# Where the streamed operand of a weight product lies in SBUF: a layer stack on one core

## The chip, the cores and the metric

The kernel runs on one core of a Trainium2 chip. The metric is the device time of one execution in microseconds; the time before is the median of three runs. One more execution was taken with the hardware profiler, and all rows of the trace come from that one.

## The reference, cut to what matters

Two transformer blocks over 256 positions of width 2048, in float32. The first block has a mixer (stick-breaking attention on 8 heads and a gated delta rule on 8 heads, joined by `w_out`), a cross attention to 256 memory positions, and a feed-forward part with a short convolution. The second has a forgetting attention (`fox`) and a sliding-window attention (`swa`). What costs the time are the products of an activation with a weight matrix:

```python
proj = h @ w_in[l]                                # 2048 x 7184
x = x + mixed @ w_out[l]                          # 2048 x 2048
u = causal_dwconv(h @ w_up, conv_w) + conv_b      # 2048 x 11264
y = (jax.nn.silu(gate) * up) @ w_down             # 5632 x 2048
p = h @ fox_w_in[j]                               # 2048 x 8224
x = x + y @ w_out                                 # 2048 x 2048, after fox and after swa
p = h @ swa_w_in[j]                               # 2048 x 4608
```

and the smaller `w_xq`, `w_xkv`, `w_xo` of the cross attention.

## The kernel before, in words

Activations lie transposed, 128 features on the partitions and 256 positions along the free axis. Every operand of a weight product is split into a high part (rounded to `float32r`) and a low part (what is left). `split` writes both parts of an activation tile side by side into one tile of 2 x 256 words, 2,048 bytes a partition. `granules` loads four such blocks of weights by one DMA of SyncE into `wt`, and ACT and DVE make the high and the low part of them in `w2`.

`linB` then makes 256 rows of a product. For each tile of the activation (index k) and each half j of the weight columns there are two matmuls: one streams all 512 columns (high and low part) of the activation tile past the high part of the weights, and one streams the 256 high columns past the low part. So the high part of the weights is loaded into TensorE once for both parts of the activation. I call the two a pair: one matmul of 512 columns, one of 256, each with its own load of 128 x 128 weights. `linA` has the operands the other way round: the activation tile is loaded and `w2` is streamed. It makes the value rows of the attentions.

The activation tiles that are streamed have four names. `xh` (made by `new_x` and `fox_x`, pool `xp`) is the normed input of a block, 16 tiles, used by every product that reads the model width. `mix` (pool `mixp`) holds the outputs of the mixers for `w_out`. `mv` (pools `mvx`, `mvf`, `mva`) holds what goes into `w_xo`, `w_down` and the two later `w_out`. `mm` is the normed memory.

Where they lie follows from the sizes. Pools are laid one behind the other in the order in which they are opened, each with its buffers one behind the other; tiles made through the class `Lined` are rounded up to multiples of 128 bytes. In front of the first pool the program keeps 16,512 bytes a partition. Pool `cp` has 25,344 bytes, pool `wp` has four `wt` of 4,096 and four `w2` of 8,192. So each `w2` begins 128 bytes behind a multiple of 256, and so does the first `xh` tile, at 91,008. An `xh` tile has room for 2,560 bytes, and `x_tile(k)` starts its 2,048 bytes 32 k bytes into it:

```python
t = xp.tile([P, 640], F32R, tag="xh", name="xh")
return t[:, 8 * k : 8 * k + 512].rearrange("p (a b) -> p a b", a=2)
```

Counted in 256s, the `xh` tiles k = 0 to 7 start at 128, 160, 192, 224, 0, 32, 64 and 96, and k = 8 to 15 again so. The tiles of `mix`, `mm` and `mv` all start at 128, as every `w2` does; the steps inside `w2` are multiples of 512 bytes and change nothing in that count.

The order of the work is the order in which the program is written, engine by engine. Side work (attention scores, the delta rule, norms) is held in generators; `tick` moves them on once for each granule of four weight blocks, so its matmuls stand between those of the weight products.

Of the kernel before, what the change touches and what calls it, by code (L numbers as in the profile page):

```python
# [9 lines left out]
F32 = mybir.dt.float32  # L10
F32R = mybir.dt.float32r
# [5 lines left out]
S, D, P = 256, 2048, 128  # L17
# [84 lines left out]
(CONSTS, CAT), (CONSTS_B, BAT), (CONSTS_L, LAT) = _consts()  # L102


LINE = 128


class Lined:
# [5 lines left out]
    def tile(self, shape, dtype, **kw):  # L114
        n, size = int(np.prod(shape[1:])), 2 if dtype == BF16 else 4
        if n * size % LINE == 0:
            return self.pool.tile(shape, dtype, **kw)
        t = self.pool.tile([shape[0], -(-n * size // LINE) * LINE // size], dtype, **kw)[:, :n]
        return t.rearrange("p (a b) -> p a b", a=shape[1]) if len(shape) == 3 else t
# [3 lines left out]
def body(ctx: ExitStack, tc: tile.TileContext, d: dict, out: bass.AP, stop=None):  # L123
# [3 lines left out]

    cp = Lined(ctx.enter_context(tc.tile_pool(name="cp", bufs=1)))
    wp = Lined(ctx.enter_context(tc.tile_pool(name="wp", bufs=4)))
    xp = Lined(ctx.enter_context(tc.tile_pool(name="xp", bufs=16)))  # L130
    sp = Lined(ctx.enter_context(tc.tile_pool(name="sp", bufs=2)))
    pl = ctx.enter_context(tc.tile_pool(name="pl", bufs=2, space=PSUM))
# [2 lines left out]
    def mm(o, lhsT, rhs, start, stop):  # L135
        nc.tensor.matmul(o, lhsT, rhs, start=start, stop=stop, skip_group_check=True)  # L136

    def side(shape, name):
        t = pside.tile([P, 512], F32, tag="side", name=name)
        n = int(np.prod(shape[1:]))  # L140
        v = t[:, :n]
        if len(shape) == 3:
            v = v.rearrange("p (a b) -> p a b", a=shape[1])
        return v

    def tt(o, a, b, op):
        vec.tensor_tensor(o, a, b, op=op)  # L147

    def stt(o, a, s, b, op0, op1):
        vec.scalar_tensor_tensor(o, a, s, b, op0=op0, op1=op1)  # L150
# [14 lines left out]
    def C(name):  # L165
        o, n = CAT[name]
        return cst[:, o : o + n]

    def V(name):
        o, n = COLS[name]  # L170
        return cols[:, o : o + n]
# [35 lines left out]
    def split(mv, src, scale=None):  # L207

        if scale is None:
            act(mv[:, 0, :], src, AF.Copy)  # L210
            tt(mv[:, 1, :], src, mv[:, 0, :].bitcast(F32), ALU.subtract)
        else:
            act(mv[:, 0, :], src, AF.Copy, scale=scale)  # L213
            stt(mv[:, 1, :], src, scale, mv[:, 0, :].bitcast(F32), ALU.mult, ALU.subtract)
# [151 lines left out]
        later("norm", work())  # L366
        return c

    def x_tile(k):

        t = xp.tile([P, 640], F32R, tag="xh", name="xh")
        return t[:, 8 * k : 8 * k + 512].rearrange("p (a b) -> p a b", a=2)

    def new_x(k, g):
        mv = x_tile(k)
        split(mv, XT[:, k, :], V(g)[:, k : k + 1])
        return mv

# [11 lines left out]
    def then(norm, g):  # L390
        xs = []

        def after(k):
            xs.append(new_x(k, g))
            norm.add(XT[:, k, :])

        return xs, after
# [6 lines left out]
    def popen(**kw):  # L404
        cm = tc.tile_pool(**kw)
        p = Lined(cm.__enter__())
        opened.append((p, cm))
        return p
# [16 lines left out]
    def first_x(k):  # L425
        n = 2 if k < 4 else 4
        if k % n == 0 and k not in made:
            src = d["xT"][k * P : (k + n) * P, :].rearrange("(k p) s -> p k s", p=P)
            nc.sync.dma_start(XT[:, k : k + n, :], src)
        if k not in made:  # L430
            made[k] = new_x(k, "mix_norm")
        return made[k]

    xh = [lambda k=k: first_x(k) for k in range(KT)]

    win = d["w_in"]
    mixpool = popen(name="mixp", bufs=16)
    mixed = [None] * 16
    gd = popen(name="gd", bufs=1)
    gates = {}  # L440
    r1 = c1 = None
# [90 lines left out]
    def gdn(hp):  # L532
        nonlocal r1, c1
        KQ = gd.tile([P, 2, 2, 256], F32, tag="KQ", name="KQ")
        if hp:
            for qk, seg in ((1, 0), (0, 1)):
                silu(KQ[:, qk], conv(linB(win, [(0, xh)], 3072 + 1024 * seg + 256 * hp), 8 * seg + 2 * hp))
        else:
            pq = linB(win, [(0, xh)], 3072, (2, 2, 4, 4, 4))
            norm0 = Norm("mix")  # L540
            later("norm", squares(norm0))
            r1 = norm0.rstd(0)
            pk = linB(win, [(0, xh)], 4096, (4, 4))
            nc.sync.dma_start(cols[:, 16:], d["cols"][:, 16:])
            tg = thin(d["w_gates"], V("mix_norm"))
        ps = linB(win, [(0, xh)], 5120 + 256 * hp)
        if hp == 0:
            silu(KQ[:, 1], conv(pq, 0))
            silu(KQ[:, 0], conv(pk, 8))
            nc.sync.dma_start(cst[:], d["consts"])  # L550
            late_constants()
            c1 = column(r1)
            later("gdn", make_gates(tg))
        v = conv(ps, 16 + 2 * hp)
        silu(v[:], v)
        ps = linB(win, [(0, xh)], 6144 + 256 * hp)
        z = t2("y", "z", 2)
        scaled(z[:], ps, r1)
        sz = t2("sz", "sz", 2)
        silu(sz[:], z)  # L560
        later("gdn", chain(hp, KQ, v, sz))

    def chain(hp, KQ, v, sz):
# [162 lines left out]
        for f in range(2):  # L726
            stt(szv[:, :, HALF[f]], ops[:, :, HALF[1 - f]], V("gdn_norm"), szv[:, :, HALF[f]], ALU.mult, ALU.mult)
        for h in range(2):
            mv = mixpool.tile([P, 2, 256], F32R, tag="mix", name="mix")
            split(mv, sz[:, h, :])  # L730
            mixed[8 + 2 * hp + h] = mv

# [13 lines left out]
    def head(hp, h, q, k, vr):  # L746
        if True:
            zt = side([P, 384], "zps")
            dg = zt.rearrange("p (a b) -> p a b", a=3)[:, 0::2, :]
            mm(zt[:, 0:256], k[:, h, 0:128], q[:, h, :], True, False)  # L750
            mm(zt[:, 256:384], k[:, h, 128:256], q[:, h, 128:256], False, False)
            e = gd.tile([P, 384], F32, tag="gt", name="sbe", bufs=4)
            spt = gd.tile([P, 384], F32, tag="gt", name="sbs", bufs=4)
            act(e[:], zt, AF.Abs)
            act(e[:], e[:], AF.Exp, scale=-1.0)
            act(e[:], e[:], AF.Ln, bias=1.0)
            stt(spt[:], zt, 0.0, e[:], ALU.max, ALU.add)
            yield
            sdg = spt[:].rearrange("p (a b) -> p a b", a=3)[:, 0::2, :]
            tt(sdg, sdg, C("sbmask").unsqueeze(1).to_broadcast([P, 2, P]), ALU.mult)  # L760
            mm(zt, C("negl"), spt[:], False, False)
            mm(zt[:, 128:256], C("negones"), spt[:, 256:384], False, False)
            mm(dg, identb[:], sbnegb.unsqueeze(1).to_broadcast([P, 2, P]), False, True)
            w = gd.tile([P, 384], F32, tag="gt", name="sbw", bufs=4)
            act(w[:], zt, AF.Exp)
            yield
            ops_ = side([P, 256], "sbo")
            mm(ops_, vr[:, 0, h * P : h * P + P], w[:, 0:256], True, False)
            mm(ops_[:, 128:256], vr[:, 1, h * P : h * P + P], w[:, 256:384], False, True)
            mv = mixpool.tile([P, 2, 256], F32R, tag="mix", name="mix")  # L770
            split(mv, ops_)
            mixed[2 * hp + h] = mv

# [3 lines left out]
    xh, after = then(norm, "xattn_norm")  # L777
# [10 lines left out]
    def new_mv():  # L788
        return mvbox[0].tile([P, 2, 256], F32R, tag="mv", name="mv")
# [25 lines left out]
    with tc.tile_pool(name="xa", bufs=2) as xa_:  # L815
# [60 lines left out]
        xh, after = then(norm, "ffn_norm")  # L876
# [15 lines left out]
    fx = []  # L892

    def fox_x(k):
        mv = x_tile(k)
        split(mv, XT[:, k, :], fg[:, k : k + 1])
        fx.append(mv)
        norm.add(XT[:, k, :])
        norm2.add(XT[:, k, :], V("final_norm")[:, k : k + 1])

    cw, cb = V("ffn_conv"), V("ffn_conv_bias")
    with tc.tile_pool(name="ff", bufs=2) as ff_:
# [15 lines left out]
        for n in range(22):  # L918
# [6 lines left out]
            for j in range(2):  # L925
                mv = new_mv()
# [9 lines left out]
    xh = fx  # L936
# [176 lines left out]
    for gidx in range(8):  # L1113
        c0 = 256 * gidx
        q = ap_.tile([P, 2, 256], F32, tag="qk", name="q")
        k = ap_.tile([P, 2, 256], F32, tag="qk", name="k")
# [23 lines left out]
    xh, after = then(norm, "norm_g_2b")  # L1140
# [40 lines left out]
    for gidx in range(8):  # L1181
# [4 lines left out]
        for j in range(2):  # L1186
# [4 lines left out]
            h = 4 * gidx + 2 * j  # L1191
# [51 lines left out]
def build(arrays, stop=None):  # L1243
    import concourse.bacc as bacc

    nc = bacc.Bacc("TRN2", target_bir_lowering=False, num_devices=1)
    d = {n: nc.dram_tensor(f"in_{n}", a.shape, F32, kind="ExternalInput").ap() for n, a in arrays.items()}
    out = nc.dram_tensor("out_0", (D, S), F32, kind="ExternalOutput").ap()
    with tile.TileContext(nc) as tc:
        body(tc, d, out, stop)  # L1250
    return nc
# [9 lines left out]
```

## Time and profile before

| what | value |
|---|---|
| time, median of three runs | 2243.81 us (2242.81 to 2244.35) |
| time of the profiled execution | 2246.18 us |
| its span, first to last instruction | 2244.3 us |
| TensorE (PE) busy | 2204.7 us, 98% of the span, 13,582 matmuls |
| loads of weights into TensorE (PEld) busy | 1904.0 us, 85% |
| VectorE (DVE) busy | 1611.4 us, 72% |
| ScalarE (ACT) busy | 1256.5 us, 56% |
| DMA engines, queue of SyncE | 53.5% |

Busy time of an engine is the time in which at least one of its instructions was under way. Matmuls overlap: one starts while the one before it still drains, so the mean duration of a matmul in a row is longer than the distance from its start to the next start. The distance between starts is what a product costs; it is read from the start of one run of matmuls to the start of the next, divided by their count.

### The profile page before, as it was taken

To read this page: it belongs to the slowest core of one execution; us is meant where nothing else is said; L and a number is where in the kernel's file an instruction comes from. 1 tells how busy PE (TensorE), PEld (TensorE's weight loads), DVE (VectorE), ACT (ScalarE), POOL (GpSimd) and SP (SyncE) were. 2 spreads that over 40 slices of the span, in tenths; PEclk is the share of its full clock that TensorE was granted. 3 is DMA by queue.
4 is the path that set the end of the run, shared out by engine and by line. 5 is a ranking of instruction groups with operands and counts; after the bars stand their busy time and mean duration, and the time that the engine had idled before them with its cause. 6 is when DMAs were issued, how large, how long until landed. Compare 5 with 4: busy or idle time off the path is not lost.

```text
span 2244.3 us, 35514 instructions
## 1 busy us (share of the span) xinstructions
PE 2204.7 (98%) x13582; PEld 1904.0 (85%) x13582; DVE 1611.4 (72%) x2681; ACT 1256.5 (56%) x2149; POOL 113.5 (5%) x161
## 2 busy tenths in 40 slices
PE   9999999999999999999999999999999999999997
PEld 7888888878878888888888888888888888888886
DVE  8757666467687766767775778867676666788775
ACT  7545555455565544544553556656556655577652
POOL 1100010000000000000000000000010000000011
PEclk9999999999999999999999999999999999999999
DMA  7443444346546566656666656555555556545453
GB/s 252 146 141 124 141 133 144 120 140 197 180 146 189 187 183 193 190 182 194 188 184 192 188 181 189 175 169 169 172 166 175 164 179 188 160 151 161 158 161 122
DMA packets 110265, 380.06 MB, mean 169 GB/s; under 512 B 11920, under 2 KB 18192, under 8 KB 110096
## 3 DMA queue, kind: packets, MB, share of 16 engines
q1 hardware_dynamic: 108720, 375.96, 53.5%
q8 instruction: 106, 1.74, 0.3%
q10 hardware_dynamic: 1232, 1.06, 0.1%
q0 software_dynamic: 144, 0.79, 0.1%
q14 instruction: 63, 0.52, 0.1%
HBM read 375.66 MB, written 2.10 MB: 168 GB/s over the span
## 4 chain that ended last, share of the span: by engine, by line
PE 92%; DVE 4%; ACT 2%; issue 1%; DMA 1%; POOL 0%; SPq 0%; DVEq 0%; ACTq 0%; POOLq 0%
PE linb L136 77%; PE lina L136 7%; PE zps L136 2%; PE yps L136 1%; PE ptps L988 1%; DVE w L147 1%; PE nps L136 1%; PE wsp L136 1%; DVE XT L150 1%; PE xps L136 1%; ACT w L258 1%; PE snp L136 0%; POOL e L506 0%; DMA MT<-in_memT 0%; PE mps L136 0%
## 5 line engine op out<-in xcount | busy, mean ns | idle before, releaser
L136 PE MATMUL linb<-xh,w 128*128 128x512 f32 x7104 | 1288.9, 340 | 12.0 <-DVE xh L150 3.0
L136 PEld LDWEIGHTS linb<-xh,w 128*128 128x128 f32 x7104 | 1091.9, 189 | 169.6 <-ACT w L258 4.4
L147 DVE TENSOR_TENSOR w<-wt,w 128x1024 fp32r<-128x1024 f32 (+2 forms) x713 | 868.3, 1220 | 325.9 <-ACT w L258 322.8
L258 ACT ACTIVATE w<-wt 128x1024 fp32r<-128x1024 f32 (+2 forms) x713 | 744.6, 1046 | 591.7 <-PE linb L136 429.3
L136 PE MATMUL linb<-mv,w 128*128 128x256 f32 (+1 forms) x2560 | 457.0, 340 | 4.4 <-DVE XT L150 4.2
L136 PEld LDWEIGHTS linb<-mv,w 128*128 128x128 f32 x2560 | 391.7, 188 | 65.9 <-issue 4.2
L136 PE MATMUL lina<-w,xh 128*128 128x512 f32 x832 | 155.2, 342 | 0.7 <-DVE w L147 0.7
L136 PEld LDWEIGHTS lina<-w,xh 128*128 128x128 f32 x832 | 128.1, 188 | 19.3 <-DVE w L147 0.9
L150 DVE SCALAR_TENSOR_TENSOR XT<-linb,XT 128x512 f32<-128x512 f32 x128 | 87.8, 690 | 32.0 <-PE linb L136 30.0
L150 DVE SCALAR_TENSOR_TENSOR y<-pre,cols,y 128x256 f32<-128x256 f32 x248 | 103.3, 479 | 0.2 <-ACT y L518 0.2
L136 PE MATMUL linb<-mix,w 128*128 128x512 f32 (+1 forms) x512 | 93.5, 342 | 1.9 <-DVE mix L147 1.9
L136 PEld LDWEIGHTS linb<-mix,w 128*128 128x128 f32 x512 | 79.6, 191 | 13.3 <-DVE mix L147 2.1
L288 ACT ACTIVATE pre<-linb 128x512 f32<-128x512 f32 x56 | 33.5, 599 | 94.9 <-PE linb L136 94.9
L150 DVE SCALAR_TENSOR_TENSOR pre<-linb,pre 128x512 f32<-128x512 f32 x56 | 38.6, 690 | 48.4 <-ACT pre L288 48.4
L912 ACT ACTIVATE y<-pre,cols 128x256 f32<-128x256 f32 x88 | 48.2, 594 | 26.7 <-DVE pre L147 26.7
L1040 POOL CAST kd<-kd 64x512 fp32r<-64x512 f32 x32 | 32.6, 1020 | 351.6 <-PE lina L136 320.8
L147 DVE TENSOR_TENSOR sqacc<-sqacc,sq 128x256 f32<-128x256 f32 x118 | 48.2, 419 | 1.4 <-DVE fg L147 0.5
L907 POOL MEMSET pre<- 128x4 f32 x44 | 4.3, 103 | 873.7 <-DVE y L150 661.3
L330 ACT ACTIVATE sq<-XT 128x256 f32<-128x256 f32 x90 | 35.5, 404 | 15.1 <-DVE XT L150 12.8
L147 DVE TENSOR_TENSOR pre<-pre,rstd 128x512 f32<-128x512 f32 x56 | 38.7, 691 | 1.6
L213 ACT ACTIVATE xh<-XT,cols 128x256 fp32r<-128x256 f32 x64 | 30.9, 500 | 8.9 <-DVE XT L150 8.8
L136 PE MATMUL zps<-kd,qs 128*128 128x256 f32 x192 | 31.3, 295 | 0.6 <-DVE qs L147 0.6
(300 smaller groups left out, 1573.7 us busy)
## 6 DMA issues: line engine op xcount, KB each, us to landing
wt<-in_w_up SPq DMA_DIRECT2D x176, 512.0 KB, 4.0
wt<-in_fox_w_in SPq DMA_DIRECT2D x128, 512.0 KB, 3.9
wt<-in_w_in SPq DMA_DIRECT2D x111, 512.0 KB, 3.6
wt<-in_swa_w_in SPq DMA_DIRECT2D x72, 512.0 KB, 3.7
wt<-in_w_down SPq DMA_DIRECT2D x64, 512.0 KB, 3.7
wt<-in_w_out SPq DMA_DIRECT2D x32, 512.0 KB, 4.3
wt<-in_fox_w_out SPq DMA_DIRECT2D x32, 512.0 KB, 3.6
wt<-in_swa_w_out SPq DMA_DIRECT2D x32, 512.0 KB, 4.5
```

Source lines behind the costliest of these rows:

```text
L136: nc.tensor.matmul(o, lhsT, rhs, start=start, stop=stop, skip_group_check=True)
L147: vec.tensor_tensor(o, a, b, op=op)
L150: vec.scalar_tensor_tensor(o, a, s, b, op0=op0, op1=op1)
L213: act(mv[:, 0, :], src, AF.Copy, scale=scale)
L258: act(wh, wt[:, h : h + n, :], AF.Copy)
L288: act(dst, ps[:, :, 1, :], AF.Copy, scale=scale)
L330: act(sq[:], src, AF.Square, scale=scale)
L907: gps.memset(pre[:, :, 0:2], 0.0)
L912: act(y[:, j, :], pre[:, j, 0:256], AF.Identity, scale=cw[:, c : c + 1], bias=cb[:, c : c + 1])
L988: nc.tensor.transpose(tps[:, b * P : b * P + P], p[:, b * P : b * P + P], ident)
L1040: gps.tensor_copy(st[e][other, i], st[e][own, i])
```

## The change

The `xh` tiles are no longer shifted inside a larger tile: each is 2,048 bytes again, and all start alike. A pool `gap` with one tile of 64 bytes a partition, which nothing reads or writes, is opened between `wp` and `xp`, so everything behind it moves. The `mix` tiles are made by a new function, which gives tile i a room of 2,304 bytes and starts it 16 i bytes into it. Nothing else is edited: no instruction is added, removed or moved.

```diff
+APART = 64
 LINE = 128
...
     wp = Lined(ctx.enter_context(tc.tile_pool(name="wp", bufs=4)))
+
+    gap = ctx.enter_context(tc.tile_pool(name="gap", bufs=1))
+    gap.tile([P, APART // 4], F32, name="gap")
     xp = Lined(ctx.enter_context(tc.tile_pool(name="xp", bufs=16)))
...
-    def x_tile(k):
-
-        t = xp.tile([P, 640], F32R, tag="xh", name="xh")
-        return t[:, 8 * k : 8 * k + 512].rearrange("p (a b) -> p a b", a=2)
-
     def new_x(k, g):
-        mv = x_tile(k)
+        mv = xp.tile([P, 2, 256], F32R, tag="xh", name="xh")
         split(mv, XT[:, k, :], V(g)[:, k : k + 1])
         return mv
...
     mixed = [None] * 16
+
+    def mix_tile(i):
+
+        t = mixpool.tile([P, 576], F32R, tag="mix", name="mix")
+        return t[:, 4 * i : 4 * i + 512].rearrange("p (a b) -> p a b", a=2)
+
...
-            mv = mixpool.tile([P, 2, 256], F32R, tag="mix", name="mix")
+            mv = mix_tile(8 + 2 * hp + h)
...
-            mv = mixpool.tile([P, 2, 256], F32R, tag="mix", name="mix")
+            mv = mix_tile(2 * hp + h)
...
     def fox_x(k):
-        mv = x_tile(k)
+        mv = xp.tile([P, 2, 256], F32R, tag="xh", name="xh")
```

## Rows read from the trace of the kernel before

**Rows 1.** The page: the span, the busy time of the engines with their shares and instruction counts, and the chain of work that ended last, by engine and by line.

```profile
span 2244.3 us, 35514 instructions
PE 2204.7 (98%) x13582; PEld 1904.0 (85%) x13582; DVE 1611.4 (72%) x2681; ACT 1256.5 (56%) x2149; POOL 113.5 (5%) x161
...
PE linb L136 77%; PE lina L136 7%; PE zps L136 2%; PE yps L136 1%; PE ptps L988 1%; DVE w L147 1%; PE nps L136 1%; PE wsp L136 1%; DVE XT L150 1%; PE xps L136 1%; ACT w L258 1%; PE snp L136 0%; POOL e L506 0%; DMA MT<-in_memT 0%; PE mps L136 0%
```

**Rows 2.** The view of waits: who waited for whom, us in total, times, the longest. The first is the split of the weights on ACT, the second the longest wait of PE.

```profile
ACT w L258 <- PE linb L136: 429.3, 294, 3.3
...
PE linb L136 <- DVE XT L150: 5.0, 4, 1.5
```

**Rows 3.** The matmuls of the weight products over the whole span, by group and shape: count, then busy us and mean ns of one, then idle us of PE before them. Those of 256 columns are as many and are left out.

```profile
L136 PE MATMUL linb<-xh,w 128*128 128x512 f32 x3552 | 1267.6, 399 | 9.5 <-DVE xh L150 3.0 <-ACT w L258 2.9 <-DVE sbk L150 2.8
...
L136 PE MATMUL linb<-mv,w 128*128 128x512 f32 x1280 | 453.1, 398 | 4.4 <-DVE XT L150 4.2
...
L136 PE MATMUL lina<-w,xh 128*128 128x512 f32 x416 | 151.0, 403 | 0.7 <-DVE w L147 0.7
...
L136 PE MATMUL linb<-mix,w 128*128 128x512 f32 x256 | 91.4, 398 | 1.9 <-DVE mix L147 1.9
...
L136 PE MATMUL linb<-mm,w 128*128 128x512 f32 x64 | 23.0, 401 | 0.0
L136 PE MATMUL lina<-w,mm 128*128 128x512 f32 x64 | 22.7, 398 | 0.0
```

**Rows 4.** The timeline of PE around ten products with `w_up`: start of a run of matmuls in us, its length, its name and its count. The second row is what follows the run.

```profile
852.98 112.03 PE L136 MATMUL linb<-xh,w 128*128 128x512 f32 x640
964.85 1.45 PE L136 MATMUL linb<-mv,w 128*128 128x512 f32 x7
```

**Rows 5.** The same timeline where all streamed tiles start at 128: `w_out` (`mix`), two stretches with `w_down`, one each with the `w_out` of fox and of swa (`mv`). Each run's row is followed by the row of what starts next; a run begins where the view's window begins.

```profile
469.80 73.66 PE L136 MATMUL linb<-mix,w 128*128 128x512 f32 x424
543.29 1.91 PE L136 MATMUL linb<-xh,w 128*128 128x512 f32 x10
...
803.76 49.39 PE L136 MATMUL linb<-mv,w 128*128 128x256 f32 x279
852.98 0.40 PE L136 MATMUL linb<-xh,w 128*128 128x512 f32 x1
...
977.65 48.70 PE L136 MATMUL linb<-mv,w 128*128 128x512 f32 x280
1026.19 1.08 PE L136 MATMUL linb<-xh,w 128*128 128x512 f32 x5
...
1811.71 81.78 PE L136 MATMUL linb<-mv,w 128*128 128x512 f32 x462
1893.33 0.87 PE L136 MATMUL linb<-xh,w 128*128 128x512 f32 x4
...
2161.72 68.08 PE L136 MATMUL linb<-mv,w 128*128 128x512 f32 x384 [1.47 <-DVE XT L150]
2229.63 0.59 PE L136 MATMUL nps<-sqacc,ones 128*128 128x256 f32 x2
```

**Rows 6.** The groups of PE in short windows. First two stretches of Rows 5 (480 to 540 us, `mix`; 808 to 850 us, `mv`). Then one product with `w_up` from 1245.1 us on, one window for each tile k, in which lie its two matmuls of 512 columns: the rows are those of k = 0 (start 128), of k = 1 and word for word of k = 5 (starts 160 and 32), of k = 2 and word for word of k = 4 and 6 (starts 192, 0 and 64), of k = 3 (224), of k = 7 (96). The last number but one is the mean ns of one.

```profile
L136 PE MATMUL linb<-mix,w 128*128 128x512 f32 x174 | 60.4, 391 | 0.0
...
L136 PE MATMUL linb<-mv,w 128*128 128x512 f32 x120 | 42.4, 399 | 0.0
...
L136 PE MATMUL linb<-xh,w 128*128 128x512 f32 x2 | 0.8, 396 | 0.0
...
L136 PE MATMUL linb<-xh,w 128*128 128x512 f32 x2 | 0.7, 394 | 0.0
...
L136 PE MATMUL linb<-xh,w 128*128 128x512 f32 x2 | 0.7, 392 | 0.0
...
L136 PE MATMUL linb<-xh,w 128*128 128x512 f32 x2 | 0.7, 397 | 0.0
...
L136 PE MATMUL linb<-xh,w 128*128 128x512 f32 x2 | 0.7, 396 | 0.0
```

**Rows 7.** The timeline of PE in the same product, at the first matmul of k = 0, 1, 2, 3 and 8: start in us, length.

```profile
1245.12 0.40 PE L136 MATMUL linb<-xh,w 128*128 128x512 f32 x1
1245.83 0.40 PE L136 MATMUL linb<-xh,w 128*128 128x512 f32 x1
1246.53 0.39 PE L136 MATMUL linb<-xh,w 128*128 128x512 f32 x1
1247.22 0.40 PE L136 MATMUL linb<-xh,w 128*128 128x512 f32 x1
...
1250.72 0.40 PE L136 MATMUL linb<-xh,w 128*128 128x512 f32 x1
```

**Rows 8.** Single tiles on DVE: count, shortest, median and longest duration in ns, first and last start, form. The first group is the short convolutions, which read `pre` at steps of 4 bytes; the second writes the low part of the `xh` tiles, at eight starts; the third writes that of the `mm` tiles, all at 128.

```profile
L150 DVE SCALAR_TENSOR_TENSOR y<-pre,cols,y x248: 469/479/485, 38.1 to 1339.1; 128x256 f32<-128x256 f32 x124
...
L150 DVE SCALAR_TENSOR_TENSOR xh<-XT,cols,xh x64: 475/479/486, 5.3 to 1896.7; 128x256 fp32r<-128x256 f32 x64
...
L150 DVE SCALAR_TENSOR_TENSOR mm<-MT,cols,mm x16: 472/478/485, 551.6 to 568.3; 128x256 fp32r<-128x256 f32 x16
```

## The prediction

> **What bounds the kernel now.** I read the page first. PE is busy for 98% of the span, and the chain that ended last lies for 77% in `linb` and 7% in `lina`, the weight products [rows 1]. The view of waits tells that nothing feeds PE too slowly: the longest wait of PE is 5.0 us in total, while the split of the weights on ACT waits 429.3 us for PE to give `w2` buffers back [rows 2]. The supply runs ahead of PE, so what a pair of matmuls (512 and 256 columns) takes is paid in full, and what it no longer takes is gained. The groups give the counts of pairs, one for each matmul of 512 columns: 3552 with `xh`, 1280 with `mv`, 256 with `mix`, 416 of `linA` with `xh`, 64 + 64 with `mm`, together 5632 [rows 3].
>
> The third view is the timeline, for the price of a pair. Around ten products with `w_up`, 640 matmuls run from 852.98 to 964.85 us without a gap: 111.87 us for 320 pairs, 349.6 ns each [rows 4]. Where all tiles start at 128, two other prices stand [rows 5]: 346.7 ns with `mix` (73.49 us for 212 pairs) and in one stretch with `w_down` (48.54 us for 140), but 352.8, 353.3 and 353.7 in the other stretches with `mv` (49.22 us for 139.5, 81.62 for 231, 67.91 for 192). So the same instructions on tiles with the same start have two steady prices, 6.6 ns or 1.9% apart. The stretches in between were entered after other work, so I take it that what came before sets which beat holds.
>
> **Does the start of a tile matter?** The windows inside one product answer it. A matmul of 512 columns has a mean of 391 ns in the stretch at 346.7 and of 399 in one at 353; with `xh` it is 396, 394, 392, 397, 392, 394, 392, 396 for k = 0 to 7 [rows 6]. The three tiles at 392 start at 192, 0 and 64: whole multiples of 64 away from the start of `w2` (128), but not on it. The tile that starts on it has 396, and the four at odd multiples of 32 have 394 to 397. The starts in time agree as far as their 10 ns go: k = 0 takes 0.71 us for its two pairs, k = 1 0.70, k = 2 0.69, and eight tiles 5.60, which is 350 a pair [rows 7]. So the price of 349.6 is a mean over tiles that differ, and the tile that starts at 192 is among the cheapest.
>
> **The change part by part.** No instruction is added or moved, so only durations can change.
>
> *Where things come to lie.* The gap of 64 bytes puts `xp` at 91,072, which is 192 counted in 256s, that is 64 bytes behind the start of every `w2` in that count. All 16 `xh` tiles then start at 192. `xp` shrinks by 16 times 512 bytes, a multiple of 256, so all later pools move to 192 as well: `mv` and `mm` start at 192, `mix` tile i at 192 + 16 i. The short title of the change says 64; by the sizes it is 64 behind a multiple of 128.
>
> *`xh` in `linB`, 3552 pairs.* Not shown before: a long run of tiles at 192. Its price lies between 345 (the 0.69 us for two pairs of k = 2 in [rows 7]) and 353.3 (the upper beat of [rows 5]). I take 346.7, because the 392 ns of tile 2 is nearest to the 391 of that beat [rows 6]. Saved: 3552 x (349.6 - 346.7) = 10.3 us.
>
> *`mv`, 1280 pairs.* The four stretches of [rows 5] are 247.29 us for 702.5 pairs, 352.0 on the mean; I let it stand for the rest. At 346.7 the saving is 1280 x 5.3 = 6.8 us; at 345 it is 9.0, at 353.3 a loss of 1.7.
>
> *`mix`, 256 pairs.* It leaves its steady 346.7 for 16 different starts. The nearest row is `xh` at eight starts, 349.6: a loss of 256 x 2.9 = 0.7 us, between 0 and 1.7 (353.3).
>
> *`linA` with `xh`, 416 pairs, and `mm`, 128.* Here `xh` is what is loaded, and no row shows such a run at one start. Between 346.7 and 353.3 against 349.6 that is -1.2 to +1.5 us; `mm` can lose 128 x 6.6 = 0.8. I take 0 for both.
>
> *The side matmuls.* PE's 2204.7 us less 5632 pairs at some 349.6 leave 236 us. Their operands move too. At the 1.9% between the two beats this is 4.5 us either way; I take 0, because operands of one pool move together.
>
> *DVE and ACT.* Tiles behind `xp` now start 64 bytes off a multiple of 128. The short convolutions read `pre` at steps of 4 bytes and all 248 lie within 469 to 485 ns; the low parts of `xh`, written at eight starts, take 479 in the median and those of `mm`, all at 128, 478 [rows 8]. So I take 0; and even 1% of DVE's 1611 us would lie under PE [rows 1, 2], whose wait for ACT and DVE is a few us.
>
> *The sum.* -10.3 - 6.8 + 0.7 = -16.4 us. In the profiled execution that is 2244.3 to 2227.9 of the span and 2246.18 to 2229.8 of its time; that execution was 2.4 us over the median. From the median: 2243.81 - 16.4 = 2227.4 us.
>
> [...] The tiles' means of 391 to 399 ns and the two beats show that a pair is delayed by something beyond its columns [rows 5, 6]. [...]
>
> **The rivals.**
>
> *The upper beat locks in (slower).* With all tiles alike nothing shakes the beat any more; a stretch that falls into 353.3 stays there, as 462 and 384 matmuls in a row did [rows 5]. For: at one common start that is where most `mv` pairs are now. Against: the start on `w2` has 396 among `xh`, 192 has 392 [rows 6]. If everything went to 353.3: `xh` 3552 x 3.7 = 13.1, `mv` 1.7, `mix` 1.7, `linA` 1.5, `mm` 0.8, together +18.8: 2262.6 us. It decides from the point at which half of the pairs of `xh` and `mv` are in the upper beat: 4832 x 6.6 = 31.9 us lie between all and none, and the gain of 16.4 is gone at 0.51.
>
> *The start is worth nothing, or the beats share the time.* The differences between the tiles of one product would be the phase that one tile hands on to the next, and long stretches at one start would fall by chance into either beat, about half and half as above. Then the time stays within some 4 us of 2244.
>
> *The gap takes no room.* Nothing uses its tile; if the allocator left it out, `xh` would start at 128, on the count of `w2`, and cost what `mv` costs: 3552 x (352.0 - 349.6) = 8.5, with `mix` 0.7: 2253 us. Against it: pools are sized by their tiles, and the class has no step that drops one.
>
> *A beat below the two.* Were 6.6 ns more to go at 192, a pair would be 340: 3552 x 9.6 + 1280 x 12.0 = 49.5 us less, 2195. For: k = 2 took 0.69 us, 345 a pair [rows 7]. Against: no steady stretch of [rows 5] has it.
>
> **How the numbers follow.** Forecast 0.59, upper beat 0.13, nothing or both beats 0.15, no gap 0.07, a lower beat 0.06. The forecast's own range: at 345 a pair `xh` and `mv` save 16.3 + 9.0, less 0.7: 2219, with the side matmuls 2214; with a quarter of the pairs in the upper beat 8.0 more, 2235, and with something from `linA` and the side 2238. The range for 8 in 10 reaches below it by a little of the lower beat, to 2212, and above it over "nothing" and "no gap", to 2256; outside are most of the upper beat and of the lower one. Below 0.2% (4.5 us), about what a measurement of this kernel can tell from no change: 0.66 faster (nearly all of the forecast, the lower beat, a little of the half-and-half), 0.14 within, 0.20 slower (upper beat, no gap).
>
> **What would show it.** In the timeline, ten products of `xh` with `w_up` in 110.9 us instead of 111.87, and every stretch of `mv` at 346.7. In the groups, the 512 column matmuls of `xh` at 391 and not 399 over such a stretch, and `linb<-mix` a little longer. The durations on DVE stay. The prediction is wrong if `xh` stretches run at 353, if their tiles still differ among each other, or if DVE or ACT gets longer and PE begins to wait for `w`.

## The result, and the profile after

The changed kernel takes 2259.57 us (median of four runs, 2256.43 to 2262.11) against 2243.31: a ratio of 1.0072, interval 1.0055 to 1.0090. It is slower by 16.3 us, where 16.4 us less was forecast. The price of a pair at which the forecast stood, 346.7 ns, is not there: every long stretch of `xh` and `mv` runs at 353.3, and `mix` at 350.9.

The page after, the span and the engines, to be read against [rows 1]:

```profile
span 2259.7 us, 35514 instructions
PE 2222.3 (98%) x13582; PEld 1913.9 (85%) x13582; DVE 1612.5 (71%) x2681; ACT 1256.9 (56%) x2149; POOL 113.6 (5%) x161
```

The count of instructions is the same. PE is busy 17.6 us longer, DVE and ACT are where they were. The view of waits, against [rows 2], first ACT, then PE:

```profile
ACT w L262 <- PE linb L140: 443.6, 302, 4.2
...
PE linb L140 <- DVE XT L154: 5.1, 4, 1.5
```

Nothing new waits in front of PE, and ACT waits 14 us longer for PE than before. So the loss is in the matmuls. The groups of the weight products by shape, against [rows 3]:

```profile
L140 PE MATMUL linb<-xh,w 128*128 128x512 f32 x3552 | 1280.9, 401 | 8.7 <-DVE xh L154 2.9 <-DVE sbk L154 2.8 <-ACT w L262 2.0
...
L140 PE MATMUL linb<-mv,w 128*128 128x512 f32 x1280 | 454.4, 397 | 4.2 <-DVE XT L154 4.1
...
L140 PE MATMUL linb<-mix,w 128*128 128x512 f32 x256 | 93.5, 405 | 1.9 <-DVE mix L151 1.9
```

The mean of an overlapping matmul tells little: `mv` went from 398 to 397 and yet costs no less, and with the 283 ns of its matmuls of 256 columns that is 680 for a pair, nearly twice the 353.3 from start to start. Prices come from starts. The timeline of PE after, the same stretches as in [rows 4, 5], each run with what follows it: ten products with `w_up`, `w_down`, the `w_out` of fox, and the first `w_out` with `mix`.

```profile
859.91 113.23 PE L140 MATMUL linb<-xh,w 128*128 128x512 f32 x640
972.98 0.40 PE L140 MATMUL linb<-mv,w 128*128 128x512 f32 x1
...
988.74 46.80 PE L140 MATMUL linb<-mv,w 128*128 128x512 f32 x264
1035.38 0.87 PE L140 MATMUL linb<-xh,w 128*128 128x512 f32 x4
...
1824.76 83.19 PE L140 MATMUL linb<-mv,w 128*128 128x512 f32 x470
1907.79 0.40 PE L140 MATMUL linb<-xh,w 128*128 128x512 f32 x1
...
474.62 74.57 PE L140 MATMUL linb<-mix,w 128*128 128x512 f32 x424
549.02 1.21 PE L140 MATMUL linb<-xh,w 128*128 128x512 f32 x6
```

`xh` takes 113.07 us for 320 pairs, 353.3 ns each instead of 349.6. `mv` takes 353.3 in both stretches (46.64 us for 132 pairs, 83.03 for 235); the first of them ran at 346.7 before. `mix`, now at sixteen starts, takes 74.40 us for 212 pairs, 350.9 instead of 346.7. With the counts of [rows 3]: 3552 x 3.7 + 1280 x 1.3 + 256 x 4.2 = 13.1 + 1.7 + 1.1 = 15.9 us. The spans differ by 15.4 us, so the longer pairs account for the loss.

That the two sums agree so closely is in part chance, because the two traces also differ in the granted clock of TensorE: on the mean it is 0.994 before and 0.992 after; in both it is 1.0 except for a few short stretches at 0.5. While matmuls run these are four before, of 3.4 to 6.8 us (from 12, 63, 463 and 562 us on), and five after; one more of some 10 us lies at the end of each, behind the last matmul. All 13,582 matmuls stand in the same order in both traces, so the distance from each start to the next can be compared one by one. Of the 15.4 us, the weight products at the clock 1.0 and without a wait have 15.0, the stretches at 0.5 have 2.5, and less waiting of PE takes 1.8 off. Single runs differ along with the granted clock too: of the four, the two at 0.997 took 2256.43 and 2257.36 us, the two at 0.992 took 2261.78 and 2262.11.

The tiles on DVE that moved off the multiples of 128 are unchanged, as [rows 8]:

```profile
L154 DVE SCALAR_TENSOR_TENSOR y<-pre,cols,y x248: 470/479/486, 39.1 to 1351.0; 128x256 f32<-128x256 f32 x124
...
L154 DVE SCALAR_TENSOR_TENSOR xh<-XT,cols,xh x64: 473/479/487, 5.5 to 1911.2; 128x256 fp32r<-128x256 f32 x64
```

### The profile page after: what moved, and what is told of

The parts are those of the page before. It is cut to its first block, busy times and chain, and to the rows that moved or that the text cites. A ratio compares the mean times of both kernels' runs of the same rounds, so it can differ in the third digit from the quotient of the medians.

```text
span 2259.7 us, 35514 instructions
## 1 busy us (share of the span) xinstructions
PE 2222.3 (98%) x13582; PEld 1913.9 (85%) x13582; DVE 1612.5 (71%) x2681; ACT 1256.9 (56%) x2149; POOL 113.6 (5%) x161
## 4 chain that ended last, share of the span: by engine, by line
PE 92%; DVE 4%; ACT 2%; DMA 1%; issue 1%; POOL 0%; SPq 0%; DVEq 0%; ACTq 0%; POOLq 0%
PE linb L140 77%; PE lina L140 7%; PE zps L140 2%; PE yps L140 1%; DVE w L151 1%; PE ptps L993 1%; PE nps L140 1%; PE wsp L140 1%; DVE XT L154 1%; PE xps L140 1%; ACT w L262 1%; PE snp L140 0%; DMA wt<-in_fox_w_in 0%; PE mps L140 0%; DVE y L154 0%
## 5 line engine op out<-in xcount | busy, mean ns | idle before, releaser
L140 PE MATMUL linb<-xh,w 128*128 128x512 f32 x7104 | 1302.4, 342 | 11.0 <-DVE xh L154 2.9
```

## The experiments

I call *distance* how far the streamed tile starts behind its block of `w2`, counted in 256s. The changed kernel has 64 throughout, the kernel before had 0 for `mv`, `mm` and `mix` and 0, 32, ... 224 in turn for `xh`. Three theories stood after the result. A: any common start of all tiles locks the upper price. B: the distance sets which prices there are. C: the place of the streamed tile alone sets them. By the price of a stretch I mean its ns for a pair. Prices below are read as above, from the ten products with `w_up` that run without a gap, unless another stretch is named.

**Other common starts.** The same kernel with other gaps.

```diff
-APART = 64
+APART = 128        # gap128; 192 in gap192; no gap at all in gap0
```

> The gap is 128 bytes instead of 64: xh, mv and mm start at 0 in 256s, 128 behind the start of w2. Theory A (any common start of all tiles locks the upper beat): 353.3 ns a pair as in the changed kernel, 2256 to 2262 us. Theory B (the distance from the start of w2 decides which beats are open): another price than 353.3 is possible here; at 346.7 the time is 2225 to 2232 us. Theory C (the start of the streamed tile itself decides, whatever w2): as B, the run with both moved tells B and C apart.

Measured 2248.15 us, ratio 1.0025 (1.0014 to 1.0035). The timeline:

```profile
852.18 112.52 PE L140 MATMUL linb<-xh,w 128*128 128x512 f32 x640
964.54 62.20 PE L140 MATMUL linb<-mv,w 128*128 128x512 f32 x352
```

112.36 us for 320 pairs, 351.1 ns: neither of the two prices known so far. A falls, since all tiles have one start here too.

> The gap is 192 bytes: xh, mv and mm start at 64 in 256s, 192 behind the start of w2. Theory A: 353.3 ns a pair, 2256 to 2262 us. Theories B and C: its own price, 346.7 (2225 to 2232 us) or 353.3.

Measured 2256.93 us, ratio 1.0064 (1.0049 to 1.0079). The same ten products go from 855.48 to 968.55 us, 353.3 ns a pair, the price of 64.

> No gap: xh, mv and mm start at 128, on the start of w2. Theory A: 353.3 ns everywhere, 2256 to 2262 us. Theories B and C: both beats occur, as they did for mv and mix before at this start (346.7 and 353.3), so between 2228 and 2258 us and some stretches at each price.

Measured 2250.34 us, ratio 1.0031 (1.0019 to 1.0042), and ten runs between 2244.75 and 2254.99. Two stretches of one execution:

```profile
848.68 113.23 PE L138 MATMUL linb<-xh,w 128*128 128x512 f32 x640
961.75 62.57 PE L138 MATMUL linb<-mv,w 128*128 128x512 f32 x352
...
1221.26 111.09 PE L138 MATMUL linb<-xh,w 128*128 128x512 f32 x640
1332.19 13.00 PE L138 MATMUL linb<-mv,w 128*128 128x512 f32 x72
```

The same matmuls on the same addresses take 353.3 ns a pair the first time and 346.7 (110.93 us for 320) the second. At the distance 0 there are two prices, and a stretch keeps the one that it fell into. That would spread the runs by 10 us; it is likely, but only this execution, the fastest of the ten, has a trace. The granted clock does not put these ten runs in order: two at 0.997 took 2248.66 and 2249.56 us, one at 0.995 took 2246.89.

**The gap ahead of the weights.** `w2` and the streamed tiles move together.

```diff
+    gap = ctx.enter_context(tc.tile_pool(name="gap", bufs=1))
+    gap.tile([P, APART // 4], F32, name="gap")
     wp = Lined(ctx.enter_context(tc.tile_pool(name="wp", bufs=4)))
-
-    gap = ctx.enter_context(tc.tile_pool(name="gap", bufs=1))
-    gap.tile([P, APART // 4], F32, name="gap")
```

> The gap of 64 bytes stands before the weight tiles: w2, xh, mv and mm all start at 192. The streamed tiles start where the changed kernel has them, the distance to w2 is 0 as without a gap. Theory A: 353.3 ns, 2256 to 2262 us. Theory B: as without a gap, stretches at 346.7 and at 353.3. Theory C: as the changed kernel, 353.3 everywhere.

Measured 2247.04 us, ratio 1.0013 (1.0000 to 1.0026), ten runs between 2236.88 and 2250.46. The streamed tiles start at 192 as in the changed kernel; the profiled execution is the fastest of the ten:

```profile
850.52 111.10 PE L141 MATMUL linb<-xh,w 128*128 128x512 f32 x640
961.45 61.49 PE L141 MATMUL linb<-mv,w 128*128 128x512 f32 x352
```

346.7 ns here, and 353.3 in other products of the same execution (with `fox_w_in`). That is the picture of the distance 0, and not that of the start 192. C falls, B stands.

**All distances in one execution.** No gap; `xh`, `mv` and `mm` start at 128, and `mix` stays spread. The tile of `w2` gets 256 bytes more, and each product shifts its content in it. The part of the edit for `w_up`, shortened:

```diff
-w2 = wp.tile([P, n, 2, 256] if inner else [P, 2, n, 256], F32R, tag="w2", ...)
+w2 = wp.tile([P, n * 512 + 64], F32R, tag="w2", ...)[:, shift[0] : shift[0] + n * 512]
+w2 = w2.rearrange("p (a b c) -> p a b c", a=n if inner else 2, c=256)
...
+shift[0] = 4 * (5 * (2 * n) % 16)
 gy = ffconv(linB(wup, [(0, xh)], 256 * n), 2 * n, "g")
+shift[0] = 4 * (5 * (2 * n + 1) % 16)
 uy = ffconv(linB(wup, [(0, xh)], 5632 + 256 * n), 44 + 2 * n, "u")
```

> All streamed tiles at 128, no gap; instead w2 is shifted from product to product inside a larger tile: in steps of 16 bytes over the 44 products with w_up, of 4 bytes (0 to 124) over the 32 with w_down, of 8 bytes (128 to 248) over the two later w_out. If the distance between the streamed tile and w2 decides, a product at 64 or 192 takes 353.3 ns a pair, at 128 351, at 0 either 346.7 or 353.3, whichever of the two operands is moved, and products at the same distance agree; the distances in between show where the cheap beat lies. If the place of the streamed tile alone decides, all products cost the same, 346.7 or 353.3.

Measured 2247.69 us in one execution. The timeline at the first matmul of each of eleven products in a row; the first ten stand at the distances 64, 240, 160, 80, 0, 176, 96, 16, 192 and 112. A product is 32 pairs, so the step from one start to the next, over 32, is the price.

```profile
853.00 0.39 PE L138 MATMUL linb<-xh,w 128*128 128x512 f32 x1
864.30 0.39 PE L138 MATMUL linb<-xh,w 128*128 128x512 f32 x1
875.40 0.40 PE L138 MATMUL linb<-xh,w 128*128 128x512 f32 x1
886.50 0.39 PE L138 MATMUL linb<-xh,w 128*128 128x512 f32 x1
897.67 0.40 PE L138 MATMUL linb<-xh,w 128*128 128x512 f32 x1
908.98 0.39 PE L138 MATMUL linb<-xh,w 128*128 128x512 f32 x1
920.27 0.42 PE L138 MATMUL linb<-xh,w 128*128 128x512 f32 x1
931.52 0.40 PE L138 MATMUL linb<-xh,w 128*128 128x512 f32 x1
942.81 0.39 PE L138 MATMUL linb<-xh,w 128*128 128x512 f32 x1
954.10 0.40 PE L138 MATMUL linb<-xh,w 128*128 128x512 f32 x1
965.29 0.39 PE L138 MATMUL linb<-mv,w 128*128 128x512 f32 x1
```

The first product takes 11.30 us, the second 11.10: 353.1 and 346.9 ns a pair, and only the place of `w2` changed between them. Over all products with `w_up`, read the same way (two or three at each distance, ns a pair):

| distance | price | distance | price |
|---|---|---|---|
| 0 | 347.1 to 353.2 | 128 | 351.1 each time |
| 16 | 352.9 | 144 | 353.2 to 353.3 |
| 32 | 346.6 to 346.7 | 160 | 346.8 to 347.0 |
| 48 | 349.8 | 176 | 352.8 to 353.5 |
| 64 | 353.1 to 353.4 | 192 | 352.9 |
| 80 | 349.1 to 349.8 | 208 | 346.8 |
| 96 | 350.0 to 351.3 | 224 | 346.8 |
| 112 | 349.5 to 349.6 | 240 | 346.7 to 347.0 |

64, 128 and 192 repeat what the gaps gave, though here the other operand was moved. By the sizes the buffers of `w2` lie 33 x 256 bytes apart here and 32 x 256 in the gap kernels, and the prices agree, which bears out counting the distance in 256s. Steps of 16 bytes change the price, as 16 (352.9), 32 (346.6 to 346.7) and 48 (349.8) show in three tries each. For smaller steps there are only the products with `w_down`, such as 347.0 at 212 and 353.3 at 216, each tried once; since one distance can have two prices, that does not show what 4 bytes do.

**The spread turned round, and with steps of 64.** Edits of the kernel before.

```diff
-return t[:, 8 * k : 8 * k + 512].rearrange("p (a b) -> p a b", a=2)
+return t[:, 8 * (15 - k) : 8 * (15 - k) + 512].rearrange("p (a b) -> p a b", a=2)   # rev
+return t[:, 16 * (k % 4) : 16 * (k % 4) + 512].rearrange("p (a b) -> p a b", a=2)   # step64
```

> The kernel before with the xh tiles spread the other way round: tile k starts 32 (15 - k) bytes into its room, so the same eight starts, in falling order. If each tile has its own price by its start, as the prediction read the windows, xh costs 349.6 ns a pair as before and the time is that of before (ratio 0.998 to 1.002). If what counts is the step from one tile to the next, the price is another one: every 1 ns of it is 3.6 us.

> The kernel before with steps of 64 bytes instead of 32: the xh tiles start at 128, 192, 0, 64 and so on. By the tiles' own durations in the windows (396, 392, 392, 392 against a mean of 394) xh gets cheaper, some 347.5 ns a pair, 2236 us. By the mean of the prices that common starts showed (350, 353.3, 350.8, 353.3) it gets dearer, 351.9, 2250 us. By the step from tile to tile: open.

Turned round: 2245.38 us, ratio 1.0008 (0.9999 to 1.0018). Its ten products cost 349.2 ns a pair (854.64 to 966.38 us) in one stretch and 351.3 (1224.31 to 1336.74) in another, so the same eight starts do not fix the price. Steps of 64: 2244.62 us, ratio 1.0005 (0.9996 to 1.0015), 350.0 a pair (853.23 to 965.24): not 347.5 as the windows promised, and not the 351.9 of the mean either.

What went wrong with the windows is seen at the tile with the distance 64. The timeline of the turned kernel at that tile and at the next, then that of the kernel with steps of 64:

```profile
1250.33 0.40 PE L136 MATMUL linb<-xh,w 128*128 128x512 f32 x1
1251.05 0.39 PE L136 MATMUL linb<-xh,w 128*128 128x512 f32 x1
```

```profile
1246.55 0.39 PE L136 MATMUL linb<-xh,w 128*128 128x512 f32 x1
1247.26 0.40 PE L136 MATMUL linb<-xh,w 128*128 128x512 f32 x1
```

Two pairs of that tile take 0.72 us when the tile before it stood at 96, and 0.71 when it stood at 0; before, behind a tile at 32, they took 0.69 [rows 7]. The changed kernel, where all stand at 64, needs 0.71. The 0.72 is from the stretch of the turned kernel at 351.3. In its stretch at 349.2 the same tile behind the same neighbour takes 0.70:

```profile
891.66 0.40 PE L136 MATMUL linb<-xh,w 128*128 128x512 f32 x1
892.36 0.39 PE L136 MATMUL linb<-xh,w 128*128 128x512 f32 x1
```

So what a tile costs in a product of mixed distances depends on the tiles before it, and at the same neighbour still on the price that the stretch has fallen into.

**The gap alone.** The kernel before with the pool `gap` added, `xh` and `mix` as they were.

```diff
     wp = Lined(ctx.enter_context(tc.tile_pool(name="wp", bufs=4)))
+
+    gap = ctx.enter_context(tc.tile_pool(name="gap", bufs=1))
+    gap.tile([P, 16], F32, name="gap")
```

> The kernel before with the gap of 64 bytes alone: xh keeps its spread (all eight starts again), mix is not spread, mv, mix and mm move to 192. If the distance decides: xh 349.6 ns as before, mv, mix and mm 353.3, so 1280 x 1.3 + 256 x 6.7 + 128 x 6.5 = 4.2 us over before, 2246.5 us, and the rest of the loss (12 us) is the xh tiles' common start.

Measured 2246.58 us, ratio 1.0013 (1.0004 to 1.0022). `xh` costs 349.7 ns (857.14 to 969.05 us): its eight distances are the same set from another beginning. So some 3 us of the loss belong to what moved behind the gap, and most of the other 13 to the common start of `xh`.

The total came as expected, but not all of its parts. `mix`, at one start with the distance 64, was expected at 353.3:

```profile
474.82 73.08 PE L139 MATMUL linb<-mix,w 128*128 128x512 f32 x418
547.73 1.44 PE L139 MATMUL linb<-xh,w 128*128 128x512 f32 x7
```

72.91 us for 209 pairs is 348.9 ns, while `mv`, at the same distance in the same execution, runs at 353.3, in the `w_out` of fox for example. The distance 64, the one of the changed kernel, thus has a second price as well. Against this 348.9 the spread of `mix` in the changed kernel, at 350.9, costs 256 x 2.0 = 0.5 us of the loss.

**The halves of the weights apart.** `xh` at 192; the two halves of `w2` shifted one at a time.

```diff
+at = (shift[0], n * 256 + 64 + shift[1])
+wh, wl = (w2[:, o : o + n * 256].rearrange("p (n c) -> p n c", n=n) for o in at)
...
+shift[:] = 0, 4 * (5 * n % 16)
 gy = ffconv(linB(wup, [(0, xh)], 256 * n), 2 * n, "g")
+shift[:] = 4 * (5 * n % 16), 0
 uy = ffconv(linB(wup, [(0, xh)], 5632 + 256 * n), 44 + 2 * n, "u")
```

> xh and mv at 192; the high and the low half of w2 have starts of their own. In the gate products with w_up the high half stays at the distance 64 and the low half goes round in steps of 16 bytes; in the up products the other way round. While the 512 columns stream past the high half, the low half is being loaded; while the 256 columns stream past the low half, the next high half is loaded. If the load of the low half under the long matmul sets the price, the gate products go through the prices of the scan (346.7 to 353.3) and the up products stay near 353.3; if the load of the high half does, the other way round; if both count, both vary. With the low half at the distance 64 too the price is 353.3 in either.

Measured 2253.70 us in one execution. As to the loads, the trace of the kernel before has one of 0.19 us that starts together with a matmul of 512 columns, both at 900.18 us, and one of 0.19 us that starts together with the matmul of 256 behind it, both at 900.42; by the order of the program each is the load for the next matmul. Both sides vary: with the high half at 64 the products go through 340.0 to 353.4 ns, with the low half at 64 through 346.6 to 353.5. One pair of distances lies below all prices seen so far. The timeline at three products in a row, the first with the high half at 64 and the low at 0, the second the other way round:

```profile
749.70 0.39 PE L140 MATMUL linb<-xh,w 128*128 128x512 f32 x1
760.58 0.40 PE L140 MATMUL linb<-xh,w 128*128 128x512 f32 x1
771.67 0.40 PE L140 MATMUL linb<-xh,w 128*128 128x512 f32 x1
```

10.88 us for 32 pairs, 340.0 ns, against 346.6. I write the two distances as (high half, low half). The second try at (64, 0), from 1293.60 to 1304.47 us, gave the same, and so did the second at (0, 64), so it matters which half lies where: both distances count. At (64, 240) the first try gave 340.6 and the second 353.1.

With both halves at 64, as in the changed kernel, the expectation of 353.3 held in one of the three products that run without a gap and failed in the two others. The first two rows are the start and the end of the one that held, the last three those of the other two, which follow each other:

```profile
671.61 0.39 PE L140 MATMUL linb<-xh,w 128*128 128x512 f32 x1
682.92 0.39 PE L140 MATMUL linb<-xh,w 128*128 128x512 f32 x1
...
1141.76 0.40 PE L140 MATMUL linb<-xh,w 128*128 128x512 f32 x1
1152.93 0.39 PE L140 MATMUL linb<-xh,w 128*128 128x512 f32 x1
1164.09 0.39 PE L140 MATMUL linb<-mv,w 128*128 128x512 f32 x1
```

11.31 us is 353.4 ns a pair; 22.33 us for the 64 pairs of the last two products is 348.9, the price that `mix` had with the gap alone. The addresses are the same in all three, so the start does not fix the price at 64 either; what ran before the products is different.

**Two distances for the whole kernel.** All four kinds of tiles at one start, none spread, by a gap of 32 or 224 bytes.

> All streamed tiles (xh, mv, mm and mix, none spread) at one start, 32 behind that of w2: a gap of 32 bytes. By the scan of distances (346.7 ns in all four products at 32) every product runs at 346.7: xh 3552 x 2.8 = 9.9 us less than before, mv 1280 x 5.2 = 6.7, linA some 1.5, so 2225 us, ratio 0.992. If a common start locks the upper beat, 2256 us or more.

Measured 2232.46 us, ratio 0.9944 (0.9932 to 0.9957), five runs between 2228.19 and 2236.29. In the profiled one, the fastest of the five:

```profile
846.33 111.10 PE L140 MATMUL linb<-xh,w 128*128 128x512 f32 x640
957.26 61.47 PE L140 MATMUL linb<-mv,w 128*128 128x512 f32 x352
```

346.7 a pair, and the same in every long stretch of `mv`. So the price is the one read from the scan; `linA` did not get faster (its matmuls of 512 columns with `xh` are busy for 150.7 us, 151.0 before). The time is a poorer match: 2225 us was expected, the median is 7 us above it, and this fastest run had a granted clock of 0.996. The other four, at 0.992 to 0.995, have no trace; the slowest, 2236.29 us, was at 0.992, so the clock can have made part of the difference.

> The same at the distance 224 (a gap of 224 bytes). In the scan three products with w_up ran at 346.7 there and one with w_down, after a stop of PE, at 352.8. If 224 has one beat as 32 has, 2225 us; if it has two as the distance 0, between 2225 and 2250 us and runs that differ.

Measured 2250.22 us, ratio 1.0026 (1.0016 to 1.0035), twelve runs between 2245.87 and 2255.34. The ten products cost 346.7 (851.85 to 962.79 us) in one stretch and 353.3 (1223.15 to 1336.22) in the next. So 224 has two prices, as the one odd product of the scan had hinted; three products at 346.8 had not been enough to tell.

**The cheapest pair of distances for the whole kernel.** The gap of 64 bytes as in the change, the low half of `w2` 64 bytes further on, `mix` not spread.

```diff
+wh, wl = (w2[:, o : o + n * 256].rearrange("p (n c) -> p n c", n=n) for o in (0, n * 256 + 16))
```

> The changed kernel's gap of 64 bytes with the low half of w2 moved 64 bytes on (and mix not spread): the high half at the distance 64, the low half at 0, the pair of distances at which one gate product ran at 340.0 ns a pair in each of its two tries. If the distances of both halves decide, linB runs at 340: against before xh 3552 x 9.5 = 33.7 us, mv 1280 x 11.9 = 15.2, mix 1.7, mm 0.5 less, so some 2193 us, ratio 0.977. If 340 is one beat of several there, something between this and 2260 us.

Measured 2214.57 us, ratio 0.9859 (0.9842 to 0.9875): faster than both kernels. The timeline, a stretch of `xh` and one of `mv`:

```profile
847.74 112.16 PE L140 MATMUL linb<-xh,w 128*128 128x512 f32 x640
959.74 60.52 PE L140 MATMUL linb<-mv,w 128*128 128x512 f32 x352
...
971.81 48.44 PE L140 MATMUL linb<-mv,w 128*128 128x512 f32 x284
1020.09 1.07 PE L140 MATMUL linb<-xh,w 128*128 128x512 f32 x5
```

350.0 in the first (112.00 us for 320 pairs) and 340.0 in the second (48.28 for 142). This pair of distances has two prices as well, 10 ns apart, and that is the larger part of why the gain is 30 us and not 51. Over all pairs of the profiled execution that directly follow a pair on tiles of the same name, the mean is 343.3 ns for `xh` and 343.0 for `mv`, against 349.3 and 351.9 before; with the counts of [rows 3] and 2.1 us for `mix` and `mm` this is a gain of some 35 us. The spans differ by 28.0 us. Of the other 7, some 3 are steps at the granted clock of 0.5 (mean 0.992 against 0.994) and some 2 are longer waits of PE; the rest was not traced to a cause.

## Why the prediction was wrong

**What bounds the kernel** held: what the pairs got longer, 15.0 us by their steps, went into the end without a new wait. **Where things come to lie** fits all runs, and DVE and ACT at nothing held (1611.4 to 1612.5 and 1256.5 to 1256.9 us busy). The gap does take its room: without it the same tiles ran at 346.7 and 353.3, with 128 bytes at 351.1.

**The step that failed is "Does the start of a tile matter?"** There I took what a tile costs inside a product of eight different starts for what it would cost in a product of tiles like it, and called the tile at 192 "among the cheapest". It is among the cheapest behind a tile at 32 less: 0.69 us there, 0.70 to 0.72 behind other tiles, 0.71 behind its like. From it came the choice of 346.7 for *`xh`* (-10.3 us; +13.1 by the timeline) and for *`mv`* (-6.8; +1.7). Both ends had been named, 345 and 353.3; the rule "the row that it is nearest to" picked the wrong one, because the 392 ns of one tile and the 391 of a steady stretch are not the same kind of number. Nor does 391 belong to the price of 346.7: the `w_down` stretch of [rows 5] at that price has a mean of 394 from 980 to 1024 us, as the tiles k = 1 and 5 have.

```profile
L136 PE MATMUL linb<-mv,w 128*128 128x512 f32 x128 | 44.4, 394 | 0.0
```

**`mix`** was right in sign and small in size: 0.7 us of loss forecast, 1.1 measured, inside its bounds.

**The rival "the upper beat locks in"** came closest: 2262.6 us against 2259.57. Its price was right, its mechanism in part. It had the same two beats, 346.7 and 353.3, open at any common start. The gaps and the scan show that the distance decides which prices are open: in long stretches only 351.1 came up at 128, only 346.7 at 32, and 353.3 and 348.9 at 64. That a stretch stays in the price that it fell into is what the runs show at 0, 64 and 224. Why all long stretches of `xh` and `mv` in the changed kernel fell into the upper price of 64 is open; at 348.9 they would have made the change a gain, by the counts of pairs an estimated 5 us. With 0.13 the rival was too low: all evidence at a common start had been at the one distance 0, and it spoke for nothing at 64. The price of the rival "a beat below the two", 340, exists, but with the low half of `w2` at another distance.

**The rival "the start is worth nothing, or the beats share the time"** had 2244 us within some 4, and the time is 2259.57. Against its first half, the place of the weights alone moved a pair between 340.0 and 353.5 ns in the execution with the halves apart.

**What stays open** is why a distance has the prices that it has, and what makes a stretch fall into one of them. The distances of both halves count, with 340.0 ns at (64, 0) and 346.6 at (0, 64); no run shows what causes the difference.

## What to carry to other kernels

The duration of one matmul inside a mixed sequence was no measure of a uniform sequence here: two pairs of the tile at 64 took 0.69 us behind one neighbour, 0.70 to 0.72 behind others and 0.71 behind their like. So make the uniform stretch and time it from start to start. Where a streamed operand and a loaded one share SBUF, scan their relative starts within one execution, repeat each place after different work and in several executions, and prefer a place that shows a single price. Here 64 looked like such a place in the trace of the changed kernel, at 353.3 ns, and was not, with 348.9 in other runs; 32 (346.7), 128 (351.1) and 192 (352.9 to 353.3) also showed one price for these products, each in a single trace.

## What the runs showed that I had not expected

The price of a pair of matmuls depends on where its two operands lie relative to each other: 340.0 to 353.3 ns in long stretches, 4%, and already in steps of 16 bytes. When both operands were moved by 64 together, the two prices of the distance 0, 346.7 and 353.3 ns, stayed. At some distances (0, 64, 224, and the pair 64 and 0) one set of addresses has two prices, kept for 64 matmuls in the shortest stretch shown and 640 in the longest. The runs of one kernel differ by 4 to 14 us, those of the kernel before by 10 (2238.45 to 2248.85 us in 23 runs beside the gaps). There the times go with the granted clock: the three runs at 0.996 or more took 2238.45 to 2241.09, the four at 0.993 or less 2244.02 to 2248.85. How much of the spread is the one and how much the other, the runs do not separate.
